# Attention steps emitted as one piece, with twice as many projection pieces behind each

## Chip, cores and metric

The kernel runs on one core of a Trainium2 chip. The metric is the device time of one execution in microseconds (us), as the median of several runs. Engines are named as in the profile: PE is the matrix engine (PEld its weight loads), DVE the vector engine, ACT the scalar engine, POOL GpSimd, SP the engine that issues most of the DMAs.

## The reference

One layer over 512 positions of width 1024, in fp32: a SwiGLU feed-forward block, a mixer, and a second feed-forward block, each between normalisations. The mixer projects its input with one matrix and feeds two groups:

```
h = prenorm(x);  p = h @ w_in          # columns: q, k, v, z, x/B/C, dt
A: a = softmax(q1 k1' + bias) - lam * softmax(q2 k2' + bias)   # causal, 8 heads
   o = rms_norm(a @ v)
B: Mamba-2 scan over 4 chunks of 128 positions, 16 heads, 2 groups; gate silu(z); norm
x = x + postnorm(concat(A, B) @ w_out)
```

## The kernel before

Products in fp32 are made of three matmuls on split operands (`mm3`: high by high, high by low, low by high, lines 210 to 214). The projection from `w_in` is cut into units: q and k of a pair of heads, z, x/B/C tiles, dt. A unit loads its weight columns, has them split (ACT line 193 makes the high part, DVE line 195 the low part), runs its matmuls into a PSUM tile named `pa`, and has them evacuated (DVE lines 503 and 506 make the low parts of q and k; 24 DMAs of SP bring q and k into the layout of attention).

While the background stream `bg` of these units is still running, attention is computed for the four pairs of heads j and four blocks of 128 queries qb: 16 steps, which this text names S00 to S33 (S12 is pair 1, block 2). A step has two halves.

- `scores` (lines 643 to 669): four matmuls of width w = 128 (qb + 1) into PSUM tiles `pb`, of which there are two buffers. DVE drains each with one operation (line 654: add the bias, write to SBUF, keep the maximum; a short second row reads the maximum). Then DVE scales the four maxima (656), ACT runs four exponentials (658), each with its sum, and DVE forms the combination coefficients (662, 663), keeps a copy of the sums (664) and combines the two maps of each head (666).
- `values` (lines 671 to 687), two steps later (depth 2): for each of two heads the probabilities are transposed on PE (680) into `pt`, ACT copies them to SBUF (681), and PE multiplies them by v (685) into `po`. This text names these T11a, T11b (transposes) and V11a, V11b (products) by step and head. After the last block of a pair, `norm` follows.

`attention` is a generator: it yields after the scores and again after the values, with the pair's number, 32 times in all. At each yield `layer` adds a number of that pair to `due` and takes as many pieces from `bg` as there are whole ones in it. A piece is the 20 to 24 projection matmuls of one unit's next part. The scan of group B (`ssd`, lines 718 to 806) then runs by `mix` over a second stream. In it, `decay` has POOL form two operands (740), PE and ACT make a decay matrix (752, 753) and DVE scales it (755); `chunk` transposes x (764), DVE scales it (766, and 777 for the state's update), PE multiplies (772, 795).

The program is recorded in this order, and a scheduler of the compiler's tile layer then puts the instructions of each engine into their final order. `mm3` keeps its first matmul behind the fifth last attention instruction (`s.fg[-s.lag]`, lag 5), so that the stream does not run ahead of attention by more than that.

Of the kernel before, what the change touches and what calls it, by code (L numbers as in the profile page):

```python
# [29 lines left out]
class Layer:  # L30
# [606 lines left out]
    def attention(s, depth, need):  # L637


        nc = s.nc  # L640
        st, s1, po = {}, {}, {}

        def scores(j, qb):
            need(j)
            qs, ks = s.qk[j, 0], s.qk[j, 1]
            if qb == 0:
                s1[j] = s.sm(8, 8, "s1")
            w = (qb + 1) * P
            e = [s.k4([P, 2, S], tag=t) for t in ("ka", "kb")]
            mx, se = s.sm(4, 4, "mx"), s.sm(4, 4, "se")  # L650
            for i in range(4):
                ps = s.pb()
                ins = nc.tensor.matmul(ps[:, :w], qs[:, i, qb * P:(qb + 1) * P], ks[:, i, :w], start=True, stop=True)  # L653
                nc.vector.tensor_tensor_reduce(out=e[i // 2][:, i % 2, :w], in0=ps[:, :w], in1=s.dist[:, S - w:], scale=1.0,
                                               scalar=-3.0e38, op0=ALU.add, op1=ALU.max, accum_out=mx[:, i:i + 1])
            nc.vector.tensor_mul(mx, mx, s.nslope[:, 4 * j:4 * j + 4])
            for i in range(4):
                nc.scalar.activation(e[i // 2][:, i % 2, :w], e[i // 2][:, i % 2, :w], AF.Exp, scale=2.0 ** -(2 * j + i // 2 + 1),
                                     bias=mx[:, i:i + 1], accum_out=se[:, i:i + 1])
            c = s.sm(2, 4, "c2")  # L660
            sv = se.rearrange("p (h m) -> p h m", m=2)
            nc.vector.reciprocal(c, sv[:, :, 1])
            nc.vector.scalar_tensor_tensor(c, c, s.nlam, sv[:, :, 0], op0=ALU.mult, op1=ALU.mult)
            nc.vector.tensor_copy(s1[j][:, 2 * qb:2 * qb + 2], sv[:, :, 0])
            for hh in range(2):
                nc.vector.scalar_tensor_tensor(e[hh][:, 0, :w], e[hh][:, 1, :w], c[:, hh:hh + 1],
                                               e[hh][:, 0, :w], op0=ALU.mult, op1=ALU.add)
            st[j, qb] = e
            s.fg.append(ins.ins)

        def values(j, qb):
            if qb == 0:
                po[j] = s.po()
            e = st.pop((j, qb))
            n = qb + 1
            for hh in range(2):
                at = s.m(tag="at")
                ps = s.pt()
                for kb in range(n):
                    nc.tensor.transpose(ps[:, kb * P:(kb + 1) * P], e[hh][:, 0, kb * P:(kb + 1) * P], s.ident)  # L680
                nc.scalar.copy(at[:, :n * P], ps[:, :n * P])
                h = 2 * j + hh
                o = po[j][:, (2 * qb + hh) * 64:(2 * qb + hh + 1) * 64]
                for kb in range(n):
                    ins = nc.tensor.matmul(o, at[:, kb * P:(kb + 1) * P], s.v[:, kb, h * 64:(h + 1) * 64],  # L685
                                           start=kb == 0, stop=kb == n - 1)
            s.fg.append(ins.ins)

        def norm(j):

            sq = s.m()
            nc.scalar.activation(sq, po[j], AF.Square)
            ms, ee = s.sm(8, 2, "ms8"), s.sm(8, 2, "ee8")
            nc.vector.tensor_reduce(ms, sq.rearrange("p (a d) -> p a d", d=64), axis=AX.X, op=ALU.add)
            nc.vector.scalar_tensor_tensor(ee, s1[j], EPS, s1[j], op0=ALU.mult, op1=ALU.mult)
            nc.vector.scalar_tensor_tensor(ms, ms, 1.0 / 64, ee, op0=ALU.mult, op1=ALU.add)
            nc.gpsimd.tensor_tensor(ms, ms, s.mhalf, op=ALU.pow)
            nc.vector.tensor_mul(s.o[:, j, :].rearrange("p (a d) -> p a d", d=64),
                                 po[j].rearrange("p (a d) -> p a d", d=64), ms.unsqueeze(2).broadcast_to([P, 8, 64]))

        steps = [(j, qb) for j in range(4) for qb in range(NT)]
        for i in range(len(steps) + depth):
            if i < len(steps):
                scores(*steps[i])
                yield steps[i][0]
            if i >= depth:
                j, qb = steps[i - depth]
                values(j, qb)
                if qb == NT - 1:
                    norm(j)  # L710
                yield j


    def to_T(s, src, col, hi, lo):
# [140 lines left out]
def layer(tc, x_d, ffn1_pre_g, ffn1_w_gate, ffn1_w_up, ffn1_w_down, ffn1_post_g, mix_pre_g, w_in,  # L855
# [3 lines left out]
    with tc.tile_pool(name="sb", bufs=1) as pool, tc.tile_pool(name="ps", bufs=8, space=PSUM) as psum, \  # L859
# [108 lines left out]

        due = 0.0
        for j in s.attention(2, need):  # L970
            due += [1.38, 1.17, 0.94, 1.07][j]
            while due >= 1.0:
                next(bg, None)
                due -= 1.0
# [83 lines left out]
```

## Time and profile before

| | |
|---|---|
| median of three runs | 1077.2 us (1074.83, 1077.2, 1077.88) |
| the profiled execution, its span | 1077.53 us, 1075.8 us |
| PE, DVE, ACT busy | 98%, 60%, 40% of the span |
| the mixer's stage that the change touches | from the dt unit (414.6 us) to 671.5 us: 256.9 us, PE busy 253.0 |

The first two rows are device times; the profile covers one execution, and everything between its span and its time lies outside the engines' records. Busy time of PE counts a matmul until its modelled end, so a PE that is 98% busy can still have short waits between matmuls, which the views of waits and the timeline show.

### The profile page before, as it was taken

The numbers are of one execution on the slowest core, as the hardware profiler recorded it, in microseconds if no ns is written. First come the engines' busy times: TensorE is split into PE (matmuls) and PEld (weight loads), VectorE is DVE, ScalarE is ACT, GpSimd is POOL, SyncE is SP. The second block draws the span as 40 slices with busy tenths as digits, with TensorE's granted clock in tenths as the row PEclk, the third lists the DMA queues.
The fourth block names the chain that finished last, engine by engine and source line by source line (L and its number), as shares of the span: only waits on it lengthen the run. The fifth ranks groups of instructions, "written<-read, shape, count | busy, mean of one in ns | idle before, by whom it ended". The sixth has DMA issues, their size and how long they took to land.

```text
span 1075.8 us, 13179 instructions
## 1 busy us (share of the span) xinstructions
PE 1056.5 (98%) x5063; PEld 876.4 (81%) x5063; DVE 649.5 (60%) x1022; ACT 427.6 (40%) x703; POOL 72.5 (7%) x92
## 2 busy tenths in 40 slices
PE   7999999999999999999999989999999999999997
PEld 6988888888888877888888768899888888888885
DVE  5347567673333754686898977683574775733344
ACT  4443233333222543466664445454332333332231
POOL 2000000000000210000023350010000000000000
PEclk9999999999999999999999999999999999999999
DMA  7231416334333344544331103232325152433312
GB/s 235 79 118 57 143 36 169 106 117 119 97 98 101 109 128 108 157 138 109 98 113 64 52 8 118 79 118 79 118 59 156 34 163 79 130 105 98 99 40 79
DMA packets 139227, 110.54 MB, mean 103 GB/s; under 512 B 5847, under 2 KB 116507, under 8 KB 139164
## 3 DMA queue, kind: packets, MB, share of 16 engines
q1 hardware_dynamic: 138588, 107.60, 33.5%
q0 software_dynamic: 576, 2.10, 0.5%
q8 instruction: 40, 0.66, 0.3%
q14 instruction: 23, 0.19, 0.1%
HBM read 99.20 MB, written 4.19 MB: 96 GB/s over the span
## 4 chain that ended last, share of the span: by engine, by line
PE 91%; DVE 4%; SPq 2%; DMA 1%; issue 1%; ACT 1%; POOL 0%; DVEq 0%; POOLq 0%; ACTq 0%
PE pa L213 21%; PE pa L214 21%; PE pa L212 17%; PE pb L367 6%; PE pa L210 4%; PE pt L367 4%; SPq L510 2%; PE po L685 2%; PE pb L213 2%; PE pb L214 2%; PE pb L212 2%; PE pa L246 1%; PE pb L311 1%; PE pb L653 1%; PE po L213 1%
## 5 line engine op out<-in xcount | busy, mean ns | idle before, releaser
L193 ACT CAST whi<-raw 128x1024 fp32r<-128x1024 f32 x188 | 196.8, 1052 | 405.7 <-PE pa L213 171.9
L195 DVE TENSOR_TENSOR wlo<-raw,whi 128x1024 fp32r<-128x1024 f32 x188 | 231.1, 1233 | 170.0 <-ACT whi L193 167.5
L213 PE MATMUL pa<-blk,whi 128*128 128x512 f32 (+1 forms) x864 | 331.0, 383 | 0.0
L214 PE MATMUL pa<-blk,wlo 128*128 128x512 f32 (+1 forms) x864 | 329.5, 383 | 0.0
L212 PE MATMUL pa<-blk,whi 128*128 128x512 f32 (+1 forms) x736 | 279.3, 380 | 0.0
L214 PEld LDWEIGHTS pa<-blk,wlo 128*128 128x128 f32 x864 | 162.4, 188 | 32.4 <-issue 1.2
L213 PEld LDWEIGHTS pa<-blk,whi 128*128 128x128 f32 x864 | 162.6, 188 | 31.2 <-issue 0.7
L212 PEld LDWEIGHTS pa<-blk,whi 128*128 128x128 f32 x736 | 138.3, 188 | 26.3
L276 DVE TENSOR_TENSOR at<-cv,pa 128x512 f32<-128x512 f32 x42 | 28.8, 686 | 110.8 <-PE pa L214 110.8
L213 PE MATMUL pa<-wlo,blk 128*128 128x512 f32 x216 | 85.2, 395 | 0.0
L214 PE MATMUL pa<-whi,blk 128*128 128x512 f32 x216 | 84.9, 397 | 0.0
L158 POOL TENSOR_TENSOR r<-r,mhalf 128x1 f32<-128x1 f32 x32 | 22.8, 712 | 753.2 <-DVE r L153 716.7
L210 PE MATMUL pa<-blk,whi 128*128 128x512 f32 x128 | 51.3, 401 | 0.0
L212 PE MATMUL pa<-whi,blk 128*128 128x512 f32 x120 | 47.5, 396 | 0.2 <-ACT blk L181 0.2
L213 PEld LDWEIGHTS pa<-wlo,blk 128*128 128x128 f32 x216 | 40.8, 189 | 8.1 <-issue 0.7
L214 PEld LDWEIGHTS pa<-whi,blk 128*128 128x128 f32 x216 | 40.4, 188 | 8.6 <-issue 0.5
L370 DVE TENSOR_TENSOR blk<-blk,pb 128x512 f32<-128x512 f32 x48 | 31.8, 682 | 21.1 <-PE pb L367 21.1
L210 PE MATMUL pa<-whi,blk 128*128 128x512 f32 x96 | 39.6, 414 | 0.2 <-ACT blk L720 0.2
L367 PE MATMUL pb<-whi,blk 128*128 128x512 f32 x96 | 31.5, 389 | 0.0
L212 PE MATMUL pb<-whi,blk 128*128 128x512 f32 x80 | 31.3, 391 | 0.0
L214 PE MATMUL pb<-whi,blk 128*128 128x512 f32 x80 | 31.1, 389 | 0.0
L213 PE MATMUL pb<-wlo,blk 128*128 128x512 f32 x80 | 31.1, 389 | 0.0
(245 smaller groups left out, 1482.9 us busy)
## 6 DMA issues: line engine op xcount, KB each, us to landing
raw<-in_ffn_w_gate_dram SPq DMA_DIRECT2D x44, 512.0 KB
raw<-in_ffn_w_up_dram SPq DMA_DIRECT2D x44, 512.0 KB
raw<-in_ffn_w_down_dram SPq DMA_DIRECT2D x44, 512.0 KB
raw<-in_w_in_dram SPq DMA_DIRECT2D x32, 512.0 KB
blk<-kc SPq DMA_DIRECT2D x96, 64.0 KB
raw<-in_w_out_dram SPq DMA_DIRECT2D x12, 512.0 KB
blk<-in_x_dram SPq DMA_DIRECT2D x4, 512.0 KB
x_d<-blk POOLq DMA_DIRECT2D x4, 512.0 KB, 3.4
```

Of the source, the lines that this page charges most:

```text
L158: s.pow = nc.gpsimd.tensor_tensor(r, r, s.mhalf[:, :1], op=ALU.pow).ins
L193: s.nc.scalar.copy(hi, raw)
L195: s.nc.vector.tensor_sub(lo, raw, hi)
L210: mm(ps, a[0], b[0], start=first, stop=False)
L212: mm(ps, a[0], b[0], start=first, stop=False)
L213: mm(ps, a[0], b[1], start=False, stop=False)
L214: return mm(ps, a[1], b[0], start=False, stop=last).ins
L276: nc.vector.tensor_mul(pr, sg, pu)
L367: nc.tensor.matmul(ps[bank, u], x, y, start=first and q == 0 and x is ah and y is wh, stop=q == 1 and x is al, skip_group_check=True)
L370: v.tensor_add(d, d, ps[bank, u])
L510: nc.sync.dma_start(st[32 * b:32 * b + 32, i, :].bitcast(F32), hl[32 * i:32 * i + 32, src, :].bitcast(F32))
L685: ins = nc.tensor.matmul(o, at[:, kb * P:(kb + 1) * P], s.v[:, kb, h * 64:(h + 1) * 64], start=kb == 0, stop=kb == n - 1)
```

## The change

`attention` yields once in an iteration, after the scores of step i and the values of step i - 2 (and the norm), where it yielded after each. There are 18 yields for 32. The four rates rise from 1.38, 1.17, 0.94, 1.07 to 2.45, 2.08, 1.67, 1.9 pieces a yield. The pieces taken over the whole of attention come to 36.48 before (32 yields at their rates) and 36.2 after: 36 whole ones each time. No operation is added or removed.

```diff
@@ -702,13 +702,12 @@
         for i in range(len(steps) + depth):
             if i < len(steps):
                 scores(*steps[i])
-                yield steps[i][0]
             if i >= depth:
                 j, qb = steps[i - depth]
                 values(j, qb)
                 if qb == NT - 1:
                     norm(j)
-                yield j
+            yield steps[min(i, len(steps) - 1)][0]
@@ -968,7 +967,7 @@
         for j in s.attention(2, need):
-            due += [1.38, 1.17, 0.94, 1.07][j]
+            due += [2.45, 2.08, 1.67, 1.9][j]
             while due >= 1.0:
                 next(bg, None)
                 due -= 1.0
```

What the scheduler makes of it is seen in the built programs. In the rows below a tile's name carries a number, and `x2` means two instructions alike in a row. Behind line 703 the changed kernel's line numbers are one lower.

**Step S13 on PE.** Before, two of S13's score matmuls (`pb`, 128x512) stand between projection matmuls, with the values V10a and V10b (`po`) behind them; 20 projection matmuls follow, and then the other two:

```order
L214 MATMUL pa_3762<-blk_2554,wlo_3699 128x512
L653 MATMUL pb_3672<-blk_3134,blk_3288 128x512
L653 MATMUL pb_3675<-blk_3134,blk_3288 128x512
L685 MATMUL po_3642<-blk_2871,at_3643 128x64
L685 MATMUL po_3642<-blk_2871,at_3648 128x64
L210 MATMUL pa_3855<-blk_2552,whi_3758 128x512
L213 MATMUL pa_3855<-blk_2553,whi_3758 128x512
L214 MATMUL pa_3855<-blk_2552,wlo_3760 128x512
```

After, all four stand together with the transposes T11a and T11b (`pt`) in between, the first score matmul of the next pair (S20, 128x128) and the values V11a and V11b right behind, and no projection matmul (`pa`) among them:

```order
L214 MATMUL pa_3855<-blk_2552,wlo_3760 128x512
L653 MATMUL pb_3691<-blk_3107,blk_3288 128x512
L653 MATMUL pb_3694<-blk_3107,blk_3288 128x512
L680 MATMUL pt_3715<-ident_63,ka_3516 128x128 x2
L680 MATMUL pt_3722<-ident_63,kb_3517 128x128 x2
L653 MATMUL pb_3697<-blk_3107,blk_3288 128x512
L653 MATMUL pb_3700<-blk_3107,blk_3288 128x512
L653 MATMUL pb_3808<-blk_3790,blk_3743 128x128
L685 MATMUL po_3629<-blk_2871,at_3714 128x64 x2
L685 MATMUL po_3629<-blk_2871,at_3721 128x64 x2
L210 MATMUL pa_3855<-blk_2554,whi_3758 128x512
```

Nine rows of attention stand in a row where four stood; 12 projection matmuls stand ahead of them, and behind them 21.

**The same place on DVE.** Before, the third and fourth drain of S12 (`pb_3612`, `pb_3615`) are followed by a normalisation (698), the scaled maxima (656) and the first drain of S13 (`pb_3672`):

```order
L654 ISA kb_3603,mx_3604<-pb_3612,dd_2811 128x384
L654 ISA mx_3604 128x1
L654 ISA kb_3603,mx_3604<-pb_3615,dd_2811 128x384
L654 ISA mx_3604 128x1
L698 TENSOR_TENSOR blk_3039<-po_3262,ms_627_3567 128x512
L656 TENSOR_TENSOR mx_3604<-mx_3604,nslope_2794 128x4
L654 ISA ka_3668,mx_3670<-pb_3672,dd_2811 128x512
L654 ISA mx_3670 128x1
L664 COPY s_595_3426<-se_3605 128x2
L654 ISA ka_3668,mx_3670<-pb_3675,dd_2811 128x512
```

After, behind the fourth drain of S12 come the two combinations of S11 (666), the low part of a weight (195), S12's maxima (656) and the low part of k2 (506), before S13's first drain (`pb_3691`):

```order
L654 ISA kb_3603,mx_3604<-pb_3615,dd_2811 128x384
L654 ISA mx_3604 128x1
L666 SCALAR_TENSOR_TENSOR ka_3516<-ka_3516,c_621_3537 128x256
L666 SCALAR_TENSOR_TENSOR kb_3517<-kb_3517,c_621_3537 128x256
L195 TENSOR_TENSOR wlo_3964<-raw_3960,whi_3962 128x1024
L656 TENSOR_TENSOR mx_3604<-mx_3604,nslope_2794 128x4
L506 TENSOR_TENSOR kc_3787<-pa_3762,kc_3787 128x512
L654 ISA ka_3687,mx_3689<-pb_3691,dd_2811 128x512
L654 ISA mx_3689 128x1
L654 ISA ka_3687,mx_3689<-pb_3694,dd_2811 128x512
L654 ISA mx_3689 128x1
L654 ISA kb_3688,mx_3689<-pb_3697,dd_2811 128x512
```

The weight's and k2's low part moved from behind S13's first two drains to ahead of them.

**Steps S23 and S30 on PE.** Before, the last two score matmuls of S23 (`pb_4095`, `pb_4098`) stand behind six transposes, and one matmul of S30 follows behind the values:

```order
L680 MATMUL pt_4196<-ident_63,ka_4012 128x128 x3
L680 MATMUL pt_4205<-ident_63,kb_4013 128x128 x3
L653 MATMUL pb_4095<-blk_3790,blk_3743 128x512
L653 MATMUL pb_4098<-blk_3790,blk_3743 128x512
L685 MATMUL po_4058<-blk_2871,at_4195 128x64 x3
L685 MATMUL po_4058<-blk_2871,at_4204 128x64 x3
L653 MATMUL pb_4159<-blk_3883,blk_3394 128x128
L210 MATMUL pa_4255<-whi_3925,blk_2552 128x512
```

After, the last three of S23 (`pb_4076` to `pb_4082`) and two of S30 (`pb_4131`, `pb_4134`) follow each other, with V21a between:

```order
L653 MATMUL pb_4076<-blk_3790,blk_3743 128x512
L653 MATMUL pb_4079<-blk_3790,blk_3743 128x512
L653 MATMUL pb_4082<-blk_3790,blk_3743 128x512
L653 MATMUL pb_4131<-blk_3941,blk_3353 128x128
L685 MATMUL po_4018<-blk_2871,at_4096 128x64 x2
L653 MATMUL pb_4134<-blk_3941,blk_3353 128x128
L685 MATMUL po_4018<-blk_2871,at_4103 128x64 x2
L210 MATMUL pa_4258<-whi_3956,blk_2552 128x512
```

Five score matmuls now come within seven rows.

**The start of the scan's second group on DVE.** Before, the decay matrix of chunk 1 is scaled (755) ahead of chunk 0's operand of the state's update (777, `kc_5188`):

```order
L748 TENSOR_TENSOR cbm_5172<-pt_5170,u_461_2762 128x128
L766 TENSOR_TENSOR kc_5188<-pt_5183,dt_3205 128x512
L769 TENSOR_TENSOR dd_5190<-pt_5183,prm_2789 128x512
L755 TENSOR_TENSOR kb_5169<-kb_5169,cbm_5172 128x1024
L777 TENSOR_TENSOR kc_5188<-kc_5188,dec_3241 128x512
```

After, that operand (line 776 there) is formed first:

```order
L765 TENSOR_TENSOR kc_5188<-pt_5183,dt_3178 128x512
L768 TENSOR_TENSOR dd_5190<-pt_5183,prm_2789 128x512
L747 TENSOR_TENSOR cbm_5172<-pt_5170,u_461_2762 128x128
L776 TENSOR_TENSOR kc_5188<-kc_5188,dec_3214 128x512
L754 TENSOR_TENSOR kb_5169<-kb_5169,cbm_5172 128x1024
```

The 128x1024 operation moved behind the 128x512 one.

## Rows read from the trace of the kernel before

**Rows 1.** The page: span, busy time of each engine, and chain by engine.
```profile
...
span 1075.8 us, 13179 instructions
...
PE 1056.5 (98%) x5063; PEld 876.4 (81%) x5063; DVE 649.5 (60%) x1022; ACT 427.6 (40%) x703; POOL 72.5 (7%) x92
...
PE 91%; DVE 4%; SPq 2%; DMA 1%; issue 1%; ACT 1%; POOL 0%; DVEq 0%; POOLq 0%; ACTq 0%
...
```

**Rows 2.** Busy time by 20 us windows (us; x instructions), granted PE clock, DMA share, GB/s.
```profile
...
420.00:440.00 20.00, 19.46 (x98) 15.95 (x97) 13.72 (x63) 7.16 (x24) 0.00 (x0) 1.00 0.41 101
...
540.00:560.00 20.00, 20.00 (x102) 16.87 (x101) 18.41 (x38) 11.64 (x26) 3.73 (x2) 1.00 0.43 133
...
600.00:620.00 20.00, 19.54 (x104) 15.22 (x103) 19.32 (x27) 10.80 (x19) 7.96 (x7) 1.00 0.24 79
620.00:640.00 20.00, 17.40 (x86) 13.19 (x84) 14.51 (x20) 7.65 (x17) 9.91 (x8) 0.91 0.00 1
...
```

**Rows 3.** Timeline of PE, 427.6 to 429.4 us: start, length, line, tiles [idle <- releaser].
```profile
...
427.58 0.40 PE L653 MATMUL pb<-blk,blk 96*128 96x256 f32 x2
428.52 0.73 PE L653 MATMUL pb<-blk,blk 96*128 96x256 f32 x2 [0.54 <-DVE mx L654]
429.09 0.40 PE L210 MATMUL pa<-blk,whi 128*128 128x512 f32 x1
429.32 0.40 PE L213 MATMUL pa<-blk,whi 128*128 128x512 f32 x1
...
```

**Rows 4.** Waits, 400 to 580 us: engine, tile, line, releaser: sum us, times, longest.
```profile
...
DVE s L664 <- ACT kb L658: 10.1, 9, 2.3
...
PEld pb L653 <- DVE mx L654: 1.3, 3, 0.7
...
PE pb L653 <- DVE mx L654: 0.8, 2, 0.5
...
PEld po L685 <- ACT at L681: 0.7, 3, 0.3
...
```

**Rows 5.** Timeline of DVE, 469.3 to 473.8 us.
```profile
...
469.30 0.49 DVE L666 SCALAR_TENSOR_TENSOR ka<-ka,c 128x256 f32<-128x256 f32 x1
469.70 0.48 DVE L666 SCALAR_TENSOR_TENSOR kb<-kb,c 128x256 f32<-128x256 f32 x1
...
471.48 1.22 DVE L195 TENSOR_TENSOR wlo<-raw,whi 128x1024 fp32r<-128x1024 f32 x1 [0.50 <-ACT whi L193]
472.62 0.74 DVE L503 SCALAR_TENSOR_TENSOR kc<-pa,qscale,kc 128x512 fp32r<-128x512 f32 x1
473.29 0.54 DVE L654 CUSTOM_DVE_ANT_0 kb<-pb,dd 128x384 f32<-128x384 f32 x1
473.76 0.08 DVE L654 DVE_READ_ACCUMULATOR2_ANT mx<- 128x1 f32 x1
...
```

**Rows 6.** Timeline of ACT, 466.5 to 475.7 us.
```profile
...
466.55 0.27 ACT L681 COPY at<-pt 128x128 f32<-128x128 f32 x1 [2.26 <-PE pt L680]
...
475.02 0.62 ACT L658 ACTIVATE ka<-ka,mx 128x384 f32<-128x384 f32 x1 [2.99 <-DVE mx L656]
...
475.64 0.60 ACT L658 ACTIVATE ka<-ka,mx 128x384 f32<-128x384 f32 x1
```

**Rows 7.** Timeline of PE, 627.3 to 632.2 us.
```profile
...
627.34 2.00 PE L772 MATMUL po<-kc,kb 128*128 128x64 f32 x16 [0.27 <-DVE kc L766]
...
632.10 2.08 PE L795 MATMUL pb<-kc,bn 128*128 128x512 f32 x2 [1.83 <-DVE kc L777]
...
```

**Rows 8.** Timeline of POOL and DVE, 629.4 to 634.7 us.
```profile
...
629.42 2.08 POOL L740 TENSOR_TENSOR kb<-u,al 128x1024 fp32r<-128x1024 f32 x1 [0.85 <-PE po L772]
...
629.66 2.38 DVE L777 TENSOR_TENSOR kc<-kc,dec 128x512 f32<-128x512 f32 x1
...
633.96 0.68 DVE L777 TENSOR_TENSOR kc<-kc,dec 128x512 f32<-128x512 f32 x1
...
```

**Rows 9.** Window 631.5 to 634.9 us, columns as in group 2.
```profile
...
631.50:634.90 3.40, 2.80 (x5) 1.57 (x6) 3.40 (x7) 0.69 (x2) 0.00 (x0) 0.51 0.00 0
...
```

## The prediction

> **What bounds the kernel now.** I began with the page: PE is busy 98% of the span and makes 91% of the chain that ended last, DVE 60%, ACT 40% [rows 1]. Only what opens or closes a gap between PE's instructions can therefore move the time; DVE and ACT count where they are late for PE. The windows show where that can be: in attention and after it PE is busy in nearly all of every 20 us, while DVE goes from 13.72 of 20 us at 420 to 18.41 at 540 and 19.32 at 600; the one large gap is at 620 to 640, where PE has 17.40 and a granted clock of 0.91 [rows 2]. Next the timeline of a place in which the kernel before already does what the change does more often, four score matmuls in a row (S01): the first two run, the other two wait 0.54 us for a buffer that DVE has to drain [rows 3]. Projection matmuls start 0.23 us apart (429.09 and 429.32). Last the waits of 400 to 580 us: over all of attention PE waits 0.8 us at score matmuls and its weight loads 1.3 us (partly the same time), and loads of the values' product wait 0.7 us for ACT [rows 4]. DVE itself waits there 10.1 us in 9 places for ACT's exponentials, at the copy of the sums (664), some 1.1 us each: such a wait holds up every drain behind it.
>
> **The change part by part.** The projection matmuls, the attention and the scan are the same operations as before, so PE's work stays; and the weights' loads are the same ones. What is new is how the rows stand. I price three clusters, the smaller places, and the scan.
>
> *Step S13 with S20 and V11.* Five score matmuls use two buffers, and PE's own time from S13's first to V11a is 5 x 0.23 and four transposes of an estimated 0.12 (16 small ones take 2.00 us in [rows 7]), together 1.6 us. DVE's drain of 384 columns takes 0.47 us from start to start [rows 5]; in proportion 512 columns take 0.63 (estimate). Count from the end of S12's last drain. DVE first does two combinations at 0.40, the weight's low part at 1.14, the maxima at 0.1, and k2's low part at about 0.67, which is what the like operation on q takes: 2.7 to 3.0 us [rows 5]. PE has 12 projection matmuls there, 2.8 us, and is at S13 at about 2.3. Drains thus end near 3.6, 4.3 and 4.9; the third score matmul, the fourth and S20 lose some 0.4 each. ACT's four exponentials of S12 (0.62 each from start to start, 2.5 in all [rows 6]) cannot start before the maxima, at 2.3, so V11's two copies end at about 5.1 and 5.4, where PE is by then. Sum 1.3 us. If DVE also comes late out of S12, because it waits there once for ACT (1.1 us, [rows 4]), it is 2.6. Rows speak for both, as 9 of 16 steps have that wait; I take 2.0.
>
> *S23 with S30.* Five score matmuls stand within seven rows. S23's fourth waits for the drain of its second, 0.5 us; S30's first for the drain of the third, 0.4; S30's second for the fourth, before which DVE has the copy of the sums of S22: 0.1, or 1.2 with the mean wait of 1.1. V21a has its copy on ACT behind S22's four exponentials (up to 0.5). Bounds 1.0 and 2.3, taken 1.8.
>
> *S31.* Its first three matmuls stand together, a fourth behind V22a and T23a. DVE meets the copy of S30's sums ahead of the first drain, and S30's exponentials stand on ACT behind the four of S23, which take an estimated 3.3 us (0.62 x 512/384, four times). One full wait for ACT was 2.3 at its longest [rows 4]; without it the drains cost 0.6. Bounds 0.6 and 2.5, taken 1.6.
>
> *Smaller places.* The decay sums of dt (line 632) now stand behind the first transposes of S00, where DVE has only just begun their input, and V02a behind a longer ACT chain: 0 to 1.0, taken 0.7. In return the group of four at S10 is spread out, which gives back about what the S01 group costs, 0.54 and a weight load's share: 0.7.
>
> Attention thus loses 2.0 + 1.8 + 1.6 + 0.7 - 0.7 = 5.4 us; the lower bounds make 2.2, the upper ones 7.7. What hides DVE's lateness elsewhere are runs of 10 to 21 projection matmuls (2.3 to 4.8 us) behind each cluster: a stall moves those back and nothing piles up.
>
> *The scan.* Before, L795 finds its operand late by 1.83 us [rows 7], because L777 took 2.38 us where its next instance takes 0.68; it began 0.24 us after POOL's L740 and ended 0.5 us after it [rows 8]. In the new order L777 comes before the 128x1024 operation. L740 still waits for the last product of chunk 0, 2.0 us behind L766's end by [rows 7], and L777 starts about 0.8 behind that end (behind 769 and 748): it is over before L740 begins. L795 then waits for ACT's copy alone, about 0.3: a gain of 1.5 to 1.8, taken 1.7. The operation behind it is needed 14 projection matmuls (3.2 us) later, which covers L740 and it.
>
> The Trainium skill ("SBUF — State Buffer", section "Who interferes with whom") says that a VectorE instruction with two SBUF inputs and a GpSimd instruction that reads SBUF exclude each other, and that the one that issues second fully blocks. The trace agrees: 631.50, where L740 ended, and 0.68 make 632.18, and L777 ended at 632.04. By that rule L777 would be free of the block whenever it begins before L740, which is the 1.7 of the sum.
>
> Right behind the 1.83 us the granted clock falls to 0.51, that is to the lower level, for 3.4 us, in which PE has 2.80 busy [rows 9]: 1.4 us lost. With the gap at 0.3 this may go; but the waits before L772 and L779 stay. I count half, 0.7, with bounds 0 and 1.4. New short waits at the end of this part (746, 719): 0 to 0.6, taken 0.5. PE's neighbours alone (a matmul of another shape behind one) make 0.3 to 0.5 more with the rows split as they now are, taken 0.4.
>
> *Sum:* 5.4 - 1.7 - 0.7 + 0.5 + 0.4 = +3.9 us on the profiled execution's 1077.53, 1081.4. The median of the runs shown is 0.3 lower, and the lowest 2.7; I say **1081.0**. Changes under 0.3%, 3.2 us, can't be told from none here. All lower bounds together give 2.2 - 1.8 - 1.4 = -1.0 (1076.2 against the median), all upper ones 7.7 - 1.5 + 0.6 + 0.5 = +7.3 (1084.5).
>
> **Rivals.**
> 1. *The clusters are short waits only; no real change.* DVE has slack where the first two clusters stand (at 540 it is busy 18.41 of 20 us, but earlier 13.72 [rows 2]), and S01 costs only 0.54 with the drains late. For it: PE's waits add to 0.8 us before though pairs of score matmuls stand everywhere. Against it: the first two clusters have a fifth matmul on the same two buffers. Attention then loses the 2.2 of the lower bounds, and 2.2 - 2.4 + 0.9 = +0.7: 1077.9.
> 2. *Faster: the whole gap at 620 to 640 goes.* If chunk 0's operands come early because attention ends earlier against the stream, the 20.00 - 17.40 = 2.6 us and the 1.4 to 1.7 of the clock there go, and 0.46 of the window before it [rows 2]: -4.7 for the -2.4 in the sum. With attention at +1.0, -3.7: 1073.5. It decides from a net loss in attention below 1.5 us. Against it: up to L772 that part stands as before.
> 3. *L777 is blocked again, or the clock falls in a cluster.* A stop like that at 630 leads to the lower clock for 3.4 us. If POOL is first, or one of the clusters reaches the 1.83 us that went before it, 1.4 to 1.7 are lost more, and both would be 1081 + 3.1 = 1084.1. For it: the clusters' upper bounds pass 1.83. Against it: they are made of waits of 0.4 with matmuls in between.
>
> **How the numbers follow.** The forecast has a chance of 0.44 (its own range 1079 to 1083; 0.31 of it above 1080.4, the rest within 0.3%), rival 1 0.27, rival 2 0.15 (0.12 below 1074.0), rival 3 0.14, all slower. That makes faster 0.12, same 0.13 + 0.27 + 0.03 = 0.43, slower 0.31 + 0.14 = 0.45. With a tenth left out at either end the range is 1074.3 to 1084.8: into rival 2 below, and past the sum of upper bounds and rival 3 above.
>
> **What would show it.** Steps right: PE waits for DVE's line 654 at S13, S20, S23, S30 and S31 that sum to 3 to 6 us, with DVE's line 664 waiting for ACT just before; L777 (776 there) of the first chunk at 0.7 us and L795 (794) waiting under 0.5; PE in the window after it near 19. Wrong: PE's waits in attention as before, under 2 us (rival 1), or a stretch at the lower clock between 430 and 580 us (rival 3). The prediction would be wrong as a whole if the scheduler's rows hid a wait that I didn't walk, such as SP's DMAs of k2 late for S20, whose order the change moves too: their landing is no term of the sum.

## The result and the profile after

The changed kernel takes 1083.51 us (median, 1082.74 to 1083.94), the kernel before in the same set 1077.54 (1074.83 to 1078.07): a ratio of 1.0061, 95% interval 1.0047 to 1.0076. It is slower by 6.0 us, more than the 3.8 that were forecast and within the range. Of the 47 runs of the kernel before that the later sets add, 16 took 1074.1 to 1075.5 us at a mean granted clock of PE of 0.998 or 0.999 and 31 took 1076.5 to 1080.2 at 0.994 to 0.997, so that its median hangs on how often PE's clock falls in it; the changed kernel's four runs are all at 0.995. Lines in the rows of the changed kernel are one lower behind 703.

The page (span, busy times, chain):

```profile
span 1081.9 us, 13180 instructions
...
PE 1059.8 (98%) x5063; PEld 877.3 (81%) x5063; DVE 653.2 (60%) x1022; ACT 427.7 (40%) x703; POOL 72.2 (7%) x92
...
PE 89%; DVE 7%; DMA 1%; ACT 1%; issue 1%; SPq 0%; DVEq 0%; POOLq 0%; POOL 0%; ACTq 0%
```

PE has 3.3 us more of busy time than in [rows 1], with the same number of instructions, and DVE's share of the chain went from 4% to 7%. The windows say where (columns as in [rows 2]):

```profile
480.00:500.00 20.00, 19.28 (x109) 16.26 (x108) 13.73 (x46) 12.68 (x34) 0.00 (x0) 0.91 0.58 153
500.00:520.00 20.00, 18.98 (x92) 15.14 (x91) 14.24 (x49) 9.93 (x31) 1.64 (x1) 1.00 0.11 29
520.00:540.00 20.00, 19.33 (x112) 16.81 (x111) 14.20 (x44) 13.25 (x35) 3.54 (x2) 1.00 0.41 108
...
600.00:620.00 20.00, 18.94 (x89) 14.38 (x87) 19.17 (x26) 8.85 (x15) 7.59 (x5) 1.00 0.16 54
620.00:640.00 20.00, 17.86 (x93) 13.52 (x94) 19.82 (x28) 9.59 (x20) 10.20 (x8) 0.93 0.08 27
```

At 480 PE has 19.28 and a granted clock of 0.91, at 500 18.98, at 520 19.33, where it had 20.00 in each of the three before; at 600 18.94, where [rows 2] have 19.54. At 620 it has 17.86 with DVE at 19.82, where [rows 2] have 17.40 and 14.51.

To put a size on each place I took, from PE's rows of both traces, the time from one start to the next, less the spacing that a matmul of that width usually has where nothing holds it up (0.228 us for 512 columns, 0.17 for 384, 0.12 for 256, 0.11 for fewer). This sum of what is lost against that spacing, called ideal here (a lower clock included), is, by part of the stage:

| part | before | after | change |
|---|---|---|---|
| attention, from the dt unit to the first product of the scan's decay (752) | 3.21 | 9.01 | +5.80 |
| scan, first group, to the first transposes of its output (719) | 2.59 | 3.46 | +0.87 |
| scan, second group | 9.47 | 9.45 | -0.02 |

The three make +6.65; the stage began 0.56 us earlier, which leaves the span's 6.1.

**Attention.** The timeline of PE at S13 and S20:

```profile
479.01 0.39 PE L214 MATMUL pa<-blk,wlo 128*128 128x512 f32 x1
479.23 0.63 PE L653 MATMUL pb<-blk,blk 96*128 96x512 f32 x2
479.70 0.38 PE L680 MATMUL pt<-ident,ka 128*128 128x128 f32 x2
479.92 0.38 PE L680 MATMUL pt<-ident,kb 128*128 128x128 f32 x2
480.47 1.11 PE L653 MATMUL pb<-blk,blk 96*128 96x512 f32 x2 [0.17 <-DVE mx L654]
482.02 0.30 PE L653 MATMUL pb<-blk,blk 96*128 96x128 f32 x1 [0.44 <-DVE s L664]
482.15 1.05 PE L685 MATMUL po<-blk,at 128*128 128x64 f32 x8
...
483.63 0.63 PE L214 MATMUL pa<-blk,wlo 128*128 128x512 f32 x1
484.06 0.63 PE L210 MATMUL pa<-blk,whi 128*128 128x512 f32 x1
```

and DVE's there:

```profile
474.96 0.17 DVE L664 COPY s<-se 128x2 f32<-128x2 f32 x1 [1.07 <-ACT kb L658]
...
477.92 1.21 DVE L195 TENSOR_TENSOR wlo<-raw,whi 128x1024 fp32r<-128x1024 f32 x1
479.05 0.15 DVE L656 TENSOR_TENSOR mx<-mx,nslope 128x4 f32<-128x4 f32 x1
479.13 0.68 DVE L506 TENSOR_TENSOR kc<-pa,kc 128x512 fp32r<-128x512 f32 x1
479.73 0.68 DVE L654 CUSTOM_DVE_ANT_0 ka<-pb,dd 128x512 f32<-128x512 f32 x1
...
480.33 0.68 DVE L654 CUSTOM_DVE_ANT_0 ka<-pb,dd 128x512 f32<-128x512 f32 x1
...
481.62 0.16 DVE L664 COPY s<-se 128x2 f32<-128x2 f32 x1
481.69 0.68 DVE L654 CUSTOM_DVE_ANT_0 kb<-pb,dd 128x512 f32<-128x512 f32 x1
```

This is what the order's rows had shown. DVE waits for ACT at a copy of the sums (474.96), comes to the weight's low part at 477.92 and to S13's first drain at 479.73, half a microsecond behind S13's first matmul; the drains then follow at 0.6 us each, with one more copy in between, and S20's matmul waits for it until 482.02. In all 1.42 us are lost up to V11. From 483.63 on the projection matmuls stand 0.43 us apart and not 0.23:

```profile
483.80:487.00 3.20, 3.20 (x10) 2.50 (x9) 1.79 (x7) 1.89 (x6) 0.00 (x0) 0.52 0.44 108
```

The granted clock is 0.52, the lower of its two levels, over these 3.2 us, and about 1.5 us go: the place as a whole loses 3.03 against ideal spacing, 1.5 of it up to V11's end. The waits in attention, as in [rows 4]:

```profile
DVE s L664 <- ACT kb L658: 13.3, 12, 2.3
...
PEld pb L653 <- DVE mx L654: 3.9, 7, 1.0
...
PE pb L653 <- DVE mx L654: 1.8, 4, 0.7
```

Score matmuls' weight loads wait 3.9 us (1.3 before), DVE's copies 13.3 (10.1). One of them holds S31:

```profile
521.92 0.17 DVE L664 COPY s<-se 128x2 f32<-128x2 f32 x1 [1.39 <-ACT kb L658]
...
522.48 0.38 PE L653 MATMUL pb<-blk,blk 96*128 96x256 f32 x1 [0.67 <-DVE mx L654]
```

DVE waited 1.39 us for ACT; the third score matmul, which needs the buffer that DVE had not drained, waited 0.67.

**The scan.** PE, DVE and POOL at the start of the second group:

```profile
620.38 1.97 PE L771 MATMUL po<-kc,kb 128*128 128x64 f32 x16 [1.45 <-DVE m L787]
...
630.52 1.90 POOL L739 TENSOR_TENSOR kb<-u,ah 128x1024 fp32r<-128x1024 f32 x1 [0.34 <-PE pb L751]
...
630.96 2.01 DVE L791 TENSOR_TENSOR blk<-blk,dd 128x512 f32<-128x512 f32 x1
...
633.22 0.66 PE L763 MATMUL pt<-ident,blk 128*128 128x128 f32 x4 [0.56 <-DVE cbm L747]
...
635.08 2.00 PE L771 MATMUL po<-kc,kb 128*128 128x64 f32 x16 [1.20 <-DVE kc L765]
...
635.74 0.68 DVE L776 TENSOR_TENSOR kc<-kc,dec 128x512 f32<-128x512 f32 x1
...
637.56 2.07 PE L794 MATMUL pb<-kc,bn 128*128 128x512 f32 x2
```

776 takes 0.68 us, as the prediction had it ([rows 8]: 2.38 for 777), and 794 has only 0.24 of extra spacing before it ([rows 7]: 1.83 of waiting). But the operation of POOL now meets another of DVE's, the gate's product 791: it took 2.01 us, from 630.96 to 632.97, beside POOL's 739 from 630.52 to 632.42. The transposes that stand behind it by DVE's queue wait (0.73 against ideal spacing), and the products 771 at 635.08 wait 1.20. Before that, at 620.38, PE waits 1.45 for DVE, which is busy throughout. And behind all this the clock falls as before: 794 takes 2.07 for two passes.

### The profile page after: what moved, and what is told of

It reads as the page before. It is cut to its first block, busy times and chain, and to the rows that moved or that the text cites. A ratio compares the mean times of both kernels' runs of the same rounds, so it can differ in the third digit from the quotient of the medians.

```text
span 1081.9 us, 13180 instructions
## 1 busy us (share of the span) xinstructions
PE 1059.8 (98%) x5063; PEld 877.3 (81%) x5063; DVE 653.2 (60%) x1022; ACT 427.7 (40%) x703; POOL 72.2 (7%) x92
## 3 DMA queue, kind: packets, MB, share of 16 engines
q1 hardware_dynamic: 138588, 107.60, 33.3%
## 4 chain that ended last, share of the span: by engine, by line
PE 89%; DVE 7%; DMA 1%; ACT 1%; issue 1%; SPq 0%; DVEq 0%; POOLq 0%; POOL 0%; ACTq 0%
PE pa L214 21%; PE pa L213 21%; PE pa L212 17%; PE pb L367 6%; PE pt L367 4%; PE pa L210 3%; PE pb L212 2%; PE pb L214 2%; PE pb L213 2%; PE po L685 1%; PE pa L246 1%; DVE cv L524 1%; PE pb L311 1%; PE po L212 1%; PE po L214 1%
## 5 line engine op out<-in xcount | busy, mean ns | idle before, releaser
L210 PE MATMUL pa<-blk,whi 128*128 128x512 f32 x120 | 48.9, 407 | 0.0
```

The lines of the kernel that those rows point to most:

```text
L210: mm(ps, a[0], b[0], start=first, stop=False)
```

## Experiments

The first seven and the last two ask what in attention costs; three ask about the scan. Medians are given with that of the kernel before in the same set.

**Where the pieces stand within a step**, in the changed kernel:

```diff
                 scores(*steps[i])
+            yield steps[min(i, len(steps) - 1)][0]
...
                     norm(j)
-            yield steps[min(i, len(steps) - 1)][0]
```

> One yield in a step as in the changed kernel, with the same rates, but between the scores and the values and not behind both. Theory (PE's loss in attention comes from score and value rows that stand together, not from the size of a portion of the stream): the rows of a step are parted again, attention loses about 5 us against ideal spacing where the change lost 9.0, and the time is 1079 to 1081. Rival (portions of twice the length are what costs, wherever they stand): attention as in the change, 1083 to 1084. The scan's order differs as well, by up to 1.5 either way.

1083.68 us (before: 1076.93; ratio 1.0064, 1.0039 to 1.0089), attention's loss 7.56. Neither expectation came out whole: a little less is lost in attention than in the change (9.01), but now at S02 (two waits of 0.9, and the lower clock behind them), S03 and S22, and the scan's first group lost 1.7 more than before. S13 and S20, which are parted here, lost 0.7 and not 3.0.

**One pair of heads with two yields again:**

```diff
                 scores(*steps[i])
+                if steps[i][0] == 1:
+                    yield 4
...
-            yield steps[min(i, len(steps) - 1)][0]
+            yield steps[min(i, len(steps) - 1)][0] if not (i < len(steps) and steps[i][0] == 1) else 4
...
-            due += [2.45, 2.08, 1.67, 1.9][j]
+            due += [2.45, 2.08, 1.67, 1.9, 1.04][j]
```

> The changed kernel with two yields a step for the second pair alone (at 1.04 pieces each, so as many pieces). Theory (S13, S20 and V11 stand together, wait 1.4 us, and the lower clock behind that costs 1.6): this 3.0 goes, the other places stay, 1080 to 1081.5. Rival (DVE's backlog in general, which only moves to the next place): 1083 to 1084. The scan can add or take 1.5.

1085.89 (1076.93; 1.0088, 1.0066 to 1.0109). S13's loss went, but S21 to S23 now had eight score matmuls in a row and lost 6.2 us with the lower clock; attention 10.34. The rival's words fit better: the place is undone and another comes up.

**Another buffer for the third score matmul:**

```diff
-                ps = s.pb()
+                ps = s.pa() if i == 2 else s.pb()
```

> The changed kernel in which the third score matmul of each step writes a buffer of the projections' tiles (three of them) and not one of the two score buffers. Theory (the two score buffers are what PE waits for): of the 3.4 us that score matmuls wait at S01, S13, S20, S23, S30, S31 some 2 go and the clock does not fall at S20 (1.6): 1079.5 to 1081.5. Rival (DVE and ACT cannot deliver faster, so values wait instead, and projections wait for their tile): 1082.5 to 1085.

1101.26 (1076.93; 1.0235, 1.0209 to 1.0261), and not for a reason that either had: the turn of the projections' tiles changed too, and the scheduler put the first scores ahead of the projections that had covered q's and k's DMAs. PE's timeline:

```profile
415.71 0.47 PE L653 MATMUL pb<-blk,blk 96*128 96x128 f32 x1 [7.22 <-DMA blk<-kc]
...
419.60 0.45 PE L653 MATMUL pa<-blk,blk 96*128 96x128 f32 x1 [1.35 <-DMA blk<-kc]
```

Attention's part began 14 us later than before. What a third score buffer alone is worth in time stays open. But the waits of its attention say what the buffers do:

```profile
PEld pb L653 <- DVE mx L654: 1.0, 1, 1.0
...
PE pb L653 <- DVE mx L654: 0.6, 1, 0.6
```

By place, 13 score matmuls stand here with at most one projection matmul between them and the second last score matmul (11 in the change), but only 4 of them take a `pb` buffer from so near. PE waits 0.6 us for a drain, in one place, where the change has 1.8 in four; the weight loads 1.0 in one for 3.9 in seven.

**The copy of the sums emitted later:**

```diff
-            nc.vector.tensor_copy(s1[j][:, 2 * qb:2 * qb + 2], sv[:, :, 0])
+            sums[j, qb] = sv
...
             e = st.pop((j, qb))
+            nc.vector.tensor_copy(s1[j][:, 2 * qb:2 * qb + 2], sums.pop((j, qb))[:, :, 0])
```

> The changed kernel in which DVE's copy of the exponentials' sums is emitted with the values, two steps later, and so does not stand waiting for ACT ahead of the next step's drains. Theory (that copy holds up drains: 1.39 us at S31, less at S20 and S30): PE's waits at score matmuls fall by about 1.5 us, and if S20's is short enough the 1.6 of the clock goes too: 1080.5 to 1082.5. Rival (the drains' own time on two buffers is all of it, and the reciprocal behind the copy waits as well): 1083 to 1084.

1084.27 (1076.93; 1.0068, 1.0042 to 1.0095). Inconclusive for the copy: the scheduler put it back ahead of S20's drain, as the releaser in the second row says (line 675 is the copy). But it shows something else, on PE:

```profile
481.09 1.11 PE L653 MATMUL pb<-blk,blk 96*128 96x512 f32 x2 [0.17 <-DVE mx L654]
482.64 0.30 PE L653 MATMUL pb<-blk,blk 96*128 96x128 f32 x1 [0.43 <-DVE s L675]
...
484.42 0.39 PE L210 MATMUL pa<-blk,whi 128*128 128x512 f32 x1
```

The waits are those of the changed kernel to 0.02 us, and the projections behind run at 0.23: here the clock did not fall. This place lost 1.51 against ideal spacing, and 3.03 in the changed kernel; attention lost 7.73. The time is no better all the same, since the clock fell twice in the scan and its second group lost 11.3 where the change loses 9.45.

**The rates alone**, two yields as before, and **the yields alone**, one a step with before's pieces for each pair:

```diff
-            due += [1.38, 1.17, 0.94, 1.07][j]
+            due += [1.225, 1.04, 0.835, 1.425][j]
```

> The kernel before, two yields a step, with rates that hand out as many pieces per pair of heads as the changed kernel does (1.225, 1.04, 0.835, 1.425). Theory (merging the yields is what makes rows stand together): attention within 2 us of the kernel before, the scan as it falls, 1076 to 1080. Rival (the kernel before is a lucky order, and any other hand-out of pieces loses the 6 us): 1082 to 1085.

```diff
-            due += [2.45, 2.08, 1.67, 1.9][j]
+            due += [2.76, 2.34, 1.88, 1.43][j]
```

> One yield a step as in the change, with as many pieces per pair of heads as the kernel before has (2.76, 2.34, 1.88, 1.43). Theory: rows still stand together at several steps, though the first pairs have more projection matmuls between them; attention loses 6 to 8 us against ideal spacing (3.2 before, 9.0 in the change), 1080 to 1083. Rival (the rates did it, fewer pieces in the first pairs): attention 3 to 5, 1077 to 1079.

The rates alone: 1080.33 (1076.77; 1.0037, 1.0018 to 1.0055), attention 5.94, with S00's matmuls nearly in a row at its start: 2.7 more than before, so neither the theory's 2 nor the rival's 6. The profile shows the fastest of its five runs, 1076.99, in which the clock did not fall, so 5.94 has no share of a lower clock in it. The yields alone: 1088.25 (1076.77; 1.0112, 1.0096 to 1.0129), attention 12.28, more than in the change itself and above what I had expected: three runs of five or six score matmuls, and the lower clock twice, for 3.2 of the 12.28. The two longest waits are not for a drain: values wait 1.28 and 1.17 us for ACT's copies (line 681).

**The suspected cost doubled**, one yield a step at the old rates:

```diff
-            due += [2.45, 2.08, 1.67, 1.9][j]
+            due += [1.38, 1.17, 0.94, 1.07][j]
```

> One yield a step with the rates of the kernel before, so that about 20 of the 36 pieces are handed out within attention and 16 behind it: the suspected cost doubled. Theory (rows that stand together wait for DVE's drains and ACT's copies, and each long stop brings the lower clock): attention loses 16 to 25 us against ideal spacing, while the scan's start has more projections to hide in: 1088 to 1098. Rival (density is no cost, PE only follows its own work): 1080 to 1085.

1109.31 (1076.77; 1.0303, 1.0273 to 1.0332), attention 33.31: more than the theory's 25, but far off the rival. About a third of it, 11.7, is lost at the lower clock, which holds for 34 us of the stage, and 4.0 while values wait for ACT's copies. The waits of score matmuls' loads alone:

```profile
PEld pb L653 <- DVE mx L654: 11.9, 23, 1.3
```

**The update's operand ahead of the next scaling**, in the kernel before:

```diff
-            v.tensor_mul(e, e, cbm.unsqueeze(1).broadcast_to([P, 8, P]))
-            return e
...
+            return e, lambda: v.tensor_mul(e, e, cbm.unsqueeze(1).broadcast_to([P, 8, P]))
...
-                v.tensor_mul(h3(xx[:, 1, :]), h3(xx[:, 0, :]), per_head(s.dec[:, n + hs.start:n + hs.stop]))
+                up = v.tensor_mul(h3(xx[:, 1, :]), h3(xx[:, 0, :]), per_head(s.dec[:, n + hs.start:n + hs.stop]))
+                with s.tc.issue_after(up.ins):
+                    scale_next()
```

> The kernel before with one order forced: DVE forms the operand of the state's update (777) ahead of scaling the next chunk's decay matrix (755), as the change has it at the start of the scan's second group; attention is as before. The prediction's term: 777 no longer meets POOL's 740, L795 is not late by 1.8, and the lower clock behind it may go: -1.7 to -3.1, 1074 to 1075.5. Rival (as the change's own trace has it, another DVE operation meets POOL and the stop stands elsewhere): within 1 us of the kernel before, 1076.5 to 1078.

1074.90 (10 runs; before 1076.77 over 14; ratio 0.9988, 0.9977 to 0.9999). The rows of DVE, POOL and PE, and a window:

```profile
618.68 1.90 POOL L740 TENSOR_TENSOR kb<-u,ah 128x1024 fp32r<-128x1024 f32 x1 [2.53 <-PE pb L752]
...
619.22 1.90 DVE L790 TENSOR_TENSOR dd<-dd,m 128x512 f32<-128x512 f32 x1
...
621.84 0.66 PE L719 MATMUL pt<-ident,blk 128*128 128x128 f32 x4 [1.88 <-DVE blk L721]
...
628.79 0.68 DVE L776 TENSOR_TENSOR kc<-kc,dec 128x512 f32<-128x512 f32 x1
...
630.41 1.95 POOL L740 TENSOR_TENSOR kb<-u,al 128x1024 fp32r<-128x1024 f32 x1 [1.71 <-PE po L771]
...
630.88 1.02 PE L796 MATMUL pb<-kc,bn 128*128 128x512 f32 x2
```

```profile
631.00:635.00 4.00, 4.00 (x18) 2.95 (x17) 3.11 (x6) 1.70 (x4) 2.11 (x3) 1.00 0.00 0
```

The operand (776 here) ends before POOL's 740 begins, PE does not wait at 796, and the clock stays at 1.00 where [rows 9] have 0.51. The second group loses 6.61 against ideal spacing and not 9.47; attention is the same (3.24). That is 2.9 in this execution and 1.9 by the medians, about the term of the sum, 1.7 and half of 1.4, but it is not that term alone. The 2.0 at 795 and the 1.4 of the lower clock went, and so did 1.4 of the 2.3 that the kernel before loses in short waits at 719, 210, 779 and 772; in their place DVE's 790 began behind another of POOL's operations, took 1.90 us for 0.68, and the transposes 719 behind it came 2.05 us late. So the rival came true as well: another operation met POOL and a stop stands elsewhere. Nor can the gain be told from the clock's: in the same set the five runs of the kernel before at 0.998 or 0.999 have a median of 1074.62.

**The gate's product out of POOL's way.** The same forced order, and the last chunk's gate of the first group, with the norm that follows it, behind the second group's first operands; in the changed kernel and in the one before:

```diff
+                    if g == 1 and c == 0:
+                        v.tensor_mul(s.gate[0], s.gate[0], s.gate[1])
...
-            v.tensor_mul(zt, zt, skip)
+            if c == NT - 1 and g == 0:
+                s.gate = (zt, skip)
+            else:
+                v.tensor_mul(zt, zt, skip)
```

> The changed kernel with its attention as it is, and two orders forced at the start of the scan's second group: the gate's product of the last chunk of the first group (791 there, which took 2.01 us beside POOL's 740) stands behind the second group's first operands, and the update's operand (776) ahead of the next chunk's scaling. Theory (in the change the scan's gain was given back because 791 met POOL and made the transposes, 0.7, and L771, 1.4, late): 2 to 3.5 us less than the change, 1080 to 1081.5. Rival (DVE has a backlog there and the stop only moves): 1082.5 to 1084.

> The same two orders in the kernel before, attention as before. Theory: as the update's operand alone (1074.9) or up to 1.5 better, since the first operands of the second group come earlier: 1073 to 1075. Rival: the gate's product, now later, holds up the next chunk: 1075 to 1077.

In the changed kernel 1079.54 (10 runs; before 1077.26 over 19; 1.0019, 1.0009 to 1.0028), 4.0 less than the change. Its rows, and two windows:

```profile
631.67 0.60 PE L762 MATMUL pt<-ident,blk 128*128 128x128 f32 x4
...
633.03 0.85 DVE L775 TENSOR_TENSOR kc<-kc,dec 128x512 f32<-128x512 f32 x1
...
633.05 2.00 PE L770 MATMUL po<-kc,kb 128*128 128x64 f32 x16 [0.68 <-DVE kc L764]
```

```profile
480.00:500.00 20.00, 19.27 (x117) 16.45 (x116) 15.23 (x50) 13.45 (x37) 0.00 (x0) 1.00 0.56 149
620.00:640.00 20.00, 18.55 (x93) 13.77 (x92) 17.39 (x26) 11.47 (x23) 10.81 (x8) 1.00 0.08 27
```

The transposes no longer wait, the products 770 wait 0.68, and the clock falls neither here nor at S13. By parts the losses are 7.50, 3.32 and 6.69: 2.8 of the gain lie in the second group, half of it the lower clock, and 1.5 in attention, whose order is that of the change, without the lower clock. Nine of the ten runs are at a mean clock of 0.998 or 0.999; against the runs of the kernel before at that clock in the same set (median 1075.4) they are 4.1 us slower, which is what the changed kernel with this order costs where the clock does not fall. In the kernel before the two orders give 1075.29 (10 runs; 1077.26; 0.9982, 0.9971 to 0.9994), no better than the first order alone: here too the operation of DVE that was 790 (795 in this kernel) met POOL (1.92 us) and 719 came 2.06 us late, and this time the clock fell behind it (0.50 for 3.4 us).

**Three yields a step**, the change's opposite:

```diff
-                values(j, qb)
+                values(j, qb, 0)
+                yield j
+                values(j, qb, 1)
...
-            due += [1.38, 1.17, 0.94, 1.07][j]
+            due += [0.92, 0.78, 0.627, 0.713][j]
```

> The kernel before with three yields a step (behind the scores and behind each head's values), rates two thirds of before's, so as many pieces: the change's opposite. Theory in its simple form (the finer the pieces are mixed in, the less stands together): attention loses 2 to 3.5 us against ideal spacing (3.2 before), 1075 to 1078. Rival (before's order is a good one by the scheduler's chance, and any other hand-out loses): attention 5 or more, 1079 to 1083.

1100.28 (1077.26; 1.0202, 1.0183 to 1.0221), attention 21.35. Here `values` also put two entries in the list that ties the stream to attention, so that this tie was tighter. With one entry:

```diff
-            s.fg.append(ins.ins)
+            if hh:
+                s.fg.append(ins.ins)
```

> Three yields a step as in the run before, but with only one entry per step for the values in the list that keeps the stream behind attention, as the kernel before has it; the run before had two, so the stream might run ahead by 1.7 steps and not 2.5. Theory (that tighter tie, not the finer mixing, made the 21.4 us of attention there): attention loses 4 to 7 us against ideal spacing, with S00's four in a row at its start, 1077 to 1081. Rival (finer mixing itself loses): attention over 12, over 1088.

1086.93 (1076.69; 1.0099, 1.0082 to 1.0116), attention 7.72, which is a little above the theory, and the scan 12.47 in its second group, which no theory had. PE starts attention with S00's four in a row and waits for DVE and for the DMAs of q or k:

```profile
421.75 0.33 PE L653 MATMUL pb<-blk,blk 96*128 96x128 f32 x1 [0.28 <-DVE mx L654]
422.99 0.46 PE L653 MATMUL pb<-blk,blk 96*128 96x128 f32 x2 [0.91 <-DMA blk<-kc]
```

The tie was most of the 21.35; but that finer mixing is better, the simple form of my theory, is not so. And no hand-out that was tried comes near the 3.2 that attention loses before: that the order of the kernel before is a good one by the scheduler's chance, the rival of three_yields, is not ruled out.

## Why the prediction came out as it did

**Attention: +5.4 forecast, +5.8 measured.** S13 with S20 and V11 2.0 against 1.42, S23 with S30 1.8 against 1.6, S31 1.6 against 1.2 (the measured ones are whole losses of the place; the kernel before loses a little there too, so they add to more than the difference). The smaller places were others than I named: the decay sums and V02a lost next to nothing, S12 and S22 lost 0.6 and 0.5. The group at S10 gave back 0.3 of the 0.7. Without the clock the difference is thus 4.3, and 1.5 come from the lower clock behind S13, which stood in rival 3 and not in the sum, where I had said that waits of 0.4 with matmuls in between speak against it. The waits were 1.1 too dear in the sum and the clock 1.5 too cheap: that the total was near is luck.

**The mechanism** is DVE's drain of two buffers, with copies that wait for ACT in its queue: the releasers of PE's waits name it (1.8 and 0.4 us at PE, 3.9 and 0.7 at its weight loads). A count from the built programs goes with it, if not in every row: score matmuls that have at most one projection matmul between them and the second last score matmul, whose buffer they take.

| kernel | such matmuls | attention's loss, us |
|---|---|---|
| before | 6 | 3.2 |
| three_yields_lag | 8 | 7.7 |
| behind_scores | 8 | 7.6 |
| pair1_split | 10 | 10.3 |
| rates_only | 11 | 5.9 |
| change | 11 | 9.0 |
| yields_only | 14 | 12.3 |
| three_yields | 17 | 21.4 |
| yields_old_rates | 36 | 33.3 |

The losses hold other things too: the lower clock took none in rates_only, three_yields_lag and before, and about 1.5 in the change and behind_scores, 3 in pair1_split and yields_only, 5 in three_yields and 12 in yields_old_rates; PE's waits for q's and k's DMAs took 3.9 in three_yields. So it isn't the number of yields that decides, but what the scheduler lets stand together; one yield a step makes it more, three make it no less. That the two buffers hold PE up in the change is seen in third_buffer, where PE's waits for drains are a third with as many matmuls as near, as far as one run with another order can show it. In other orders ACT's copies are the larger part: in yields_only values wait 2.4 us for them and score matmuls 1.1 for drains.

**The scan: -1.5 forecast, +0.85 measured. This is the step that failed.** Its own row came as worked out: 776 at 0.68 us, and the wait at 794 gone but for 0.24 (a gain of 1.75 for 1.7). What failed is "the waits before L772 and L779 stay". In the change DVE is busy 19.82 of 20 us there, the gate's product met POOL's operation instead, and 1.6 (771 at 620), 0.7 (763) and 0.4 (771 at 635, beyond what 779 and 772 lost before) came up, while 1.1 that the kernel before loses at 719 and 210 from 617 to 621 went. I had followed the one pair that collided before and not asked what of DVE's stands beside POOL's 740 in the new order. It is the same with the order alone, in the kernel before: 790 met POOL there, and 1.9 us by the medians are what is left. With the gate moved away, the second group's loss falls from 9.45 to 6.69. The clock, of which I had counted half, fell all the same. New short waits, 0.5 by the sum, were 0.8 in the first group, at 745, which waits for ACT, and 771, which waits for DVE.

**Rivals.** Rival 1 fell by PE's waits in attention; rival 2 by the window at 620; rival 3's fall of the clock came true once, at S13, and its other half, 777 blocked again, came true with another operation in 777's place. The forecast's sign held, and so did its mechanism in attention; the scan's gain did not come, and the size was 3.8 for 6.0. (The sum of the lower bounds leaves out the 0.3 of PE's neighbours: it is -0.7, not -1.0.)

**A version better than both**, by the medians, is update_before_scale, the kernel before with one order forced: 1074.90 for 1076.77, with an interval that ends at 0.9999. That it is better where the clock does not fall is not shown.

## What to carry to other kernels

When a change moves the hand-out of filler work, read the built order of the engine that drains the shared buffers, not the number of hand-outs: count the uses that come back to a buffer with too little work in between. When a collision between two engines goes, look up what that operation and its neighbours meet in the new order before booking the gain, and look again in the trace that follows: here each order that took one collision away brought another. And force the one order that matters by a dependence, since the scheduler undoes an edit that only changes where it is written (here the copy of the sums).

## What was not expected of the hardware

The lower clock doesn't follow from a given wait. The same rows with the same 1.42 us of waits at S13 brought 3.2 us at 0.52 in the changed kernel and none in sums_copied_late and gate_late_in_change; and in rates_only PE's wait at 795 was 1.99 against ideal spacing, as before, with a granted clock of 1.00 over that window. At 719 a wait of 1.88 us in update_before_scale was followed by none and one of 1.89 in gate_late_in_before by 3.4 us at 0.50. Rival 3 of the prediction took the fall for a consequence of such a stop; but runs of one and the same kernel differ in it. What decides is open.

POOL's operations of 128x1024 held up different ones of DVE's: 777 beside 740 (2.38 us for 0.68), 791 beside 739 in the change (2.01 for 0.68), 790 beside 740 in update_before_scale (1.90 for 0.68), 794 beside 739 in gate_late_in_change (1.25 for 0.68); each began after POOL's and ended 0.5 us behind it. The Trainium skill ("SBUF — State Buffer", section "Who interferes with whom") gives the rule that of a VectorE instruction with two SBUF inputs and a GpSimd instruction that reads SBUF the one that issues second fully blocks; these rows agree. A DVE operation that began first was not lengthened: in the kernel before 755 began at 628.52, 0.90 us ahead of 740, ran into it and took 1.23 us, as against 1.21 at 625.08.
